# First layer's experts: fourteen scatter-added in memory and two summed on chip, in place of twelve and four

## The chip, the cores and the metric

The kernel runs on one core of a Trainium2 chip. The metric is the device time of one execution in microseconds, as the median of several runs. The core has a matrix engine (TensorE, PE in the rows), a vector engine (VectorE, DVE), a scalar engine (ScalarE, ACT), GpSimd (POOL) and SyncE (SP), which here issues most of the loads. Each engine works through its own list of instructions in order and waits on semaphores for the others. Data move between memory and the on-chip SBUF by DMA; TensorE writes into PSUM, from which VectorE and ScalarE read.

## The reference, cut to what matters

Two layers work on 512 latent tokens and 256 context tokens of width 1024. Each has an attention half and then a mixture of 16 experts in which every expert chooses its own tokens: 64 of the latent and 32 of the context, the context only in the first layer. The expert's rows are scaled and added back into the stream at the chosen places:

```python
def ec_ffn(h, router_w, w_gate, w_up, w_down):
    cap = EC_CAPACITY_FACTOR * n_tok // N_EXPERTS
    aff = jax.nn.softmax((h @ router_w).astype(jnp.float32), axis=-1)
    top_aff, idx = lax.top_k(jnp.swapaxes(aff, 1, 2), cap)
    xg = jax.vmap(lambda hb, ib: hb[ib])(h, idx)
    hid = jax.nn.silu(einsum(xg, w_gate)) * einsum(xg, w_up)
    y = einsum(hid, w_down) * top_aff[..., None].astype(h.dtype)
    return zeros((n_tok, d)).at[idx.reshape(-1)].add(y.reshape(-1, d))
...
xl = xl + g2 * ec_ffn(rmsnorm(xl, norm2_g) * (1 + sc2) + sh2, ...)
```

The context gets the same update (`xc`) in the first layer. The last step of the whole is a norm of the latent stream.

## The kernel before

The change lies in the expert stage of the first layer (`upd` is true there). The stream stands in SBUF as six tiles `X` of 128 tokens by 1024: four latent (`xl`), two context (`xc`). A copy of it was written to memory as `acc` while the tokens were routed (L860).

The experts' weights come through a ring of slots of 1 MB each; SyncE issues the loads, and a slot comes free when TensorE has used it. An expert takes four slots for gate and up (`load_gu`) and two for down (`load_d`).

The loop over `e` from 0 to 16 (L1172) overlaps the experts. One iteration gives TensorE, in this order, which is written out by hand: `gate_up(e, 1)` and `gate_up(e, 0)` (context, then latent rows); `down(e-1, 0)`; the transposes of the next expert's gathered rows (`columns(e+1)`); the transposes of the hidden rows (`hid_t(e, 1)`, `hid_t(e, 0)`), which ScalarE copies to SBUF as `hTe`; up to six pieces of the combine that stood in the list `todo` when the iteration began; `down(e-1, 1)`. The order on the other engines is not written out: a planner sets it, by the order of emission, priorities and its own costs.

What follows `down` differs. For `e < in_dram`, 12 in the first layer, VectorE scales the product's rows into a tile `ya` of 96 rows (two instructions latent, four context), and GpSimd issues a DMA that adds these rows into `acc` at the tokens' places (L1076). For the last four experts the rows are summed on chip. The latent rows become `yt`, and of it `yp`: ScalarE casts the leading part (L1086) and VectorE subtracts it for the remainder (L1087); `yp` has two buffers. GpSimd builds a one-hot tile `pl` of the chosen tokens (`places`, L1103), and TensorE multiplies `pl` with `yp`: each pair of experts gives eight pieces, four token blocks by two halves, of two matmuls each, and VectorE adds each piece into `X` (L1120). The context rows of four experts are gathered in one tile `y` and split into `yc` (`split`), and give four pieces of two matmuls. The pair (12, 13) stands in `todo` from iteration 14 on, so its pieces are multiplied in iterations 15 and 16; the pair (14, 15) and the context come last.

In iteration 14 all of `X` is loaded anew from `acc`, by six DMAs on GpSimd (L1194). A one-column copy of the next expert's `xgT` into each tile (L1193) stands ahead of them, so that they don't run earlier. After the last additions the second layer begins with the norms of the six tiles (L141, L142, L309), which need all of `X`.

Of the kernel before, what the change touches and what calls it, by code (L numbers as in the profile page):

```python
# [10 lines left out]
F32R = mybir.dt.float32r  # L11
# [8 lines left out]
D = 1024  # L20
# [6 lines left out]
NE = 16  # L27
# [17 lines left out]
def hybrid_kernel(ctx: ExitStack, tc: tile.TileContext, a, out):  # L45
    nc = tc.nc
    V, S, G, PE, Q = nc.vector, nc.scalar, nc.gpsimd, nc.tensor, nc.sync

    def early(n):

        def wrap(f):
            def g(*args, **kw):
                with tc.high_priority(n):
                    return f(*args, **kw)
            return g
        return wrap
# [39 lines left out]
    def ps_mm():  # L96
        return psn("mm")

    def ps_tp():
        return psn("tp")  # L100
# [30 lines left out]
    @early(-400)  # L131
    def parts(x, out, hi=None, sub=V):

        (hi or V.tensor_copy)(out[0], x)  # L134
        sub.tensor_tensor(out[1], x, out[0].bitcast(F32), op=OP.subtract)  # L135
# [13 lines left out]
    acc = dram.tile([NT, D], F32, name="acc")  # L149
# [83 lines left out]
    X = {}  # L233

    def layer(li, ada):
        upd = li == 0
# [539 lines left out]
        for r in range(len(streams)):  # L776
            t = rt.tile([128, D], F32, name=f"g1_{r}")
# [6 lines left out]
        for r, grp in enumerate(streams):  # L784
            t = rt.tile([48, len(grp) * 64], F32, name=f"affT{r}")
# [92 lines left out]
        class Choice:  # L878
# [22 lines left out]
            def finish(self):  # L901
                r, cap, np_ = self.r, caps[self.r], nparts[self.r]
                rows = 128 // np_
                v0, v1 = self.val[0:NE], rt.tile([NE, cap], F32, name="mgv")
                V.tensor_copy(v1, self.val[32:48, ::-1])
                lt = rt.tile([NE, 2, 128], F32, name="lt")
                i0, i1, ge = [rt.tile([NE, cap], F32, name=f"mg{i}") for i in range(3)]

                def wide(x):
                    return x[:, None, :].to_broadcast([NE, np_, cap])  # L910

                V.tensor_scalar(i0, self.idx[0:NE], -4.0 * cap, None, op0=OP.add)
                V.tensor_copy(i1, self.idx[32:48, ::-1])
                V.tensor_tensor(ge, v0, v1, op=OP.is_ge)
                V.tensor_tensor(i0, i0, i1, op=OP.subtract)
                V.tensor_tensor(i0, i0, ge, op=OP.mult)
                lw = [lt[:, i].rearrange("p (q c) -> p q c", q=np_) for i in range(2)]
                V.scalar_tensor_tensor(lw[0], wide(i1), 4.0 * cap, wide(i0), op0=OP.add, op1=OP.add)
                V.tensor_tensor(lw[1], wide(v0), wide(v1), op=OP.max)
                ps = ps_tp()  # L920
                for i in range(2):
                    PE.transpose(ps[:, i * NE:(i + 1) * NE], lt[:, i, :], ident[:NE, :NE])

                if r == 1:
                    V.tensor_scalar(gidx[64:96], ps[64:96, :NE], float(NL), None, op0=OP.add)
                    st = mods.tile([128, NE // np_], F32, name=f"st{r}")
                    for q in range(np_):
                        V.tensor_copy(st[q * rows:(q + 1) * rows, :], ps[q * rows:(q + 1) * rows, q:NE:np_])
                else:
                    if upd:  # L930
                        V.tensor_copy(gidx[:64], ps[:64, :NE])
                    else:
                        for q in range(2):
                            V.tensor_copy(gidx[64 * q:64 * q + 64, :NE // 2], ps[64 * q:64 * q + 64, q:NE:2])
                    st = mods.tile([128, NE], F32, name=f"st{r}")
                    V.tensor_copy(st, ps[:, :NE])
                slots.append(st)
                w = mods.tile([128, NE], F32, name=f"gw{r}")
                V.tensor_copy(w, ps[:, NE:2 * NE])
                gw.append(w)  # L940
# [38 lines left out]
        ex = pool(es_x, f"ex{li}", 2, side="right")  # L979
# [9 lines left out]
        xgs, xgTs = {}, {}  # L989
# [65 lines left out]
        Y = {}  # L1055

        def down(e, r):
            wd, hT = wds[e], hTs[e, r]
            ps = ps_mm()
            np_ = nparts[r]  # L1060
            n, rows = D // np_, 128 // np_
            for k in range(4):
                o = k * 64 if r == 0 else (k % 2) * 64 + (k // 2) * 32
                for q in range(np_):
                    mm(ps[rows * q:rows * (q + 1), :n], hT[:, o:o + rows], wd[k][:, q * n:(q + 1) * n], k == 0, k == 3)
            if e < in_dram:

                if r == 0:
                    Y["rows"] = ex.tile([ng, D], F32, name="ya")
                t = Y["rows"]  # L1070
                for q in range(np_):
                    own = slice(rows * q, rows * (q + 1))
                    V.scalar_tensor_tensor(t[64 * r:64 * r + rows, q * n:(q + 1) * n], ps[own, :n], gw[r][own, e:e + 1],
                                           g2[r][own, :], op0=OP.mult, op1=OP.mult)
                if r == 1:
                    G.indirect_dma_start(out=acc, out_offset=bass.IndirectOffsetOnAxis(ap=gidx[:ng, e:e + 1], axis=0),  # L1076
                                         in_=t, in_offset=None, compute_op=OP.add)
                return
            if r == 0:

                t = ex.tile([128, 512], F32, name="yt", bufs=1)
                V.scalar_tensor_tensor(t, ps, gw[0][:, e:e + 1], g2[0], op0=OP.mult, op1=OP.mult)  # L1082
                y = ex.tile([128, 2, 512], F32R, name="yp", bufs=2 if upd else 3)
                for q in range(2):
                    own, other = slice(64 * q, 64 * q + 64), slice(64 - 64 * q, 128 - 64 * q)
                    S.copy(y[own, q], t[own])  # L1086
                    V.tensor_tensor(y[other, q], t[own], y[own, q].bitcast(F32), op=OP.subtract)  # L1087
                Y[0] = y
                return

            i = e % np_
            if i == 0:
                Y[r] = ex.tile([128, D], F32, name=f"y{r}", bufs=1)
            for q in range(np_):
                V.scalar_tensor_tensor(Y[r][i * rows:(i + 1) * rows, q * n:(q + 1) * n], ps[rows * q:rows * (q + 1), :n],
                                       gw[r][rows * q:rows * (q + 1), e:e + 1], g2[r][rows * q:rows * (q + 1), :],
                                       op0=OP.mult, op1=OP.mult)

        def places(r, g):

            nt = NL if r == 0 else NCX
            pl = ex.tile([128, nt], F32R, name=f"pl{r}", bufs=2 - r)
            G.tensor_scalar(pl, tok[:, :nt], slots[r][:, g:g + 1], None, op0=OP.is_equal)  # L1103
            return pl

        def split(g):

            o = [ex.tile([128, D], F32R, name=f"yc{i}", bufs=1) for i in range(2)]
            parts(Y[1], o, S.copy)
            pl = places(1, g)  # L1110
            return [(pl, [y[:, hf * 512:(hf + 1) * 512] for hf in range(2)]) for y in o]

        def combine(r, terms):
# [12 lines left out]
        rs = range(len(streams))  # L1126
        todo, pair = [], []

        in_dram = 12 if upd else 0

        def finish(e, r):
            down(e, r)
# [39 lines left out]
        for e in range(NE + 1):  # L1172
            ready = len(todo)
            if e + 1 < NE and e + 1 not in wgus:
                load_gu(e + 1, G if upd and e == 1 else Q)
            if e < NE:
                if e not in wds:
                    load_d(e, Q if upd or e > 1 else G)
                for r in reversed(rs):
                    gate_up(e, r)  # L1180
            if e and upd:
                finish(e - 1, 0)
            elif e:
                hid_t(e - 1, 0)
            if e < NE:
                if e + 1 < NE:
                    columns(e + 1)
                if e + 2 < NE:
                    gather(e + 2)
                if upd and e == NE - 2:  # L1190

                    for i, t in enumerate(X["xl"] + X["xc"]):
                        V.tensor_copy(t[:, 0:1], xgTs[NE - 1][:, 0, 0:1])  # L1193
                        G.dma_start(t, acc[i * 128:(i + 1) * 128, :])  # L1194
                if upd:
                    for r in reversed(rs):
                        hid_t(e, r)
            fill(min(ready, 6 if upd else 4))
            if e:
                for r in rs[1:] if upd else rs:  # L1200
                    finish(e - 1, r)
        if upd:
            fill(len(todo))
        else:
            final(todo, ex)
# [104 lines left out]
```

## Time and profile before

| what | value |
|---|---|
| time, median of 3 runs | 1432.83 us (1432.7 to 1435.84) |
| time of the profiled execution | 1436.76 us |
| its span, first to last instruction | 1435.0 us |
| mean granted clock of TensorE | 0.958 |
| TensorE busy (matmul) | 1284.1 us, 89% |
| VectorE busy | 710.2 us, 49% |
| ScalarE busy | 513.5 us, 36% |
| GpSimd busy | 216.7 us, 15% |
| moved by DMA | 321.16 MB, 224 GB/s over the span |

The profile is that of one execution, with times from the start of its span. A busy TensorE is not one at its peak, since matmuls are pipelined and their ends modelled. The granted clock is that of TensorE as a share of its full 2.4 GHz. "x96" counts instructions that were merged into one row; a matmul in f32 appears as two. "[2.26 <-ACT hTe L1053]" is idle time of the engine ahead of a row and what ended it.

### The profile page before, as it was taken

What the parts mean: (1) busy time and instruction counts of PE and PEld (TensorE: products, weight loads), DVE (VectorE), ACT (ScalarE), POOL (GpSimd) and SP (SyncE); (2) the same over time, 40 slices, a digit from 0 to 9 for tenths busy, and PEclk for the clock granted to TensorE, in tenths of its full rate; (3) what the DMA queues carried; (4) which work ended last, traced back from release to release, by engine and by line L of the source; (5) the groups of instructions that cost most, each with busy time, mean ns of one, the idle gap of its engine ahead of it and who ended that gap; (6) DMA issues with size and microseconds to landing.
All of it is one profiled execution on the core that took longest, in us unless ns stands there. A gap on an engine that the chain in (4) does not pass through costs nothing. (4 is left out here: it accounts for less than half of the span.)

```text
span 1435.0 us, 21605 instructions
## 1 busy us (share of the span) xinstructions
PE 1284.1 (89%) x8598; PEld 811.0 (57%) x8598; DVE 710.2 (49%) x1564; ACT 513.5 (36%) x1093; POOL 216.7 (15%) x252
## 2 busy tenths in 40 slices
PE   3989989989999959999999959998999968999986
PEld 0768866656678833444443438876778754343332
DVE  1545266566653453333333484847876352333435
ACT  2523145455543322222222143436666232232222
POOL 1111001313120230111110120101232011111201
PEclk9989999999999979999999989999999988999998
DMA  9523416535661389999999610210016447999993
GB/s 359 190 88 118 161 40 235 184 132 195 246 235 54 138 313 363 374 375 376 374 374 389 243 57 32 72 63 1 2 35 258 163 190 303 419 420 419 420 421 124
DMA packets 54084, 321.16 MB, mean 224 GB/s; under 512 B 8528, under 2 KB 8656, under 8 KB 20448
## 3 DMA queue, kind: packets, MB, share of 16 engines
q1 hardware_dynamic: 45664, 286.75, 51.2%
q0 software_dynamic: 8320, 33.03, 7.2%
q8 instruction: 68, 1.11, 0.3%
q14 instruction: 32, 0.26, 0.1%
HBM read 304.52 MB, written 15.24 MB: 223 GB/s over the span
## 5 line engine op out<-in xcount | busy, mean ns | idle before, releaser
L59 PE MATMUL mm<-slot,xgT 128*32 128x256 f32 (+1 forms) x2048 | 289.1, 492 | 5.6 <-DMA slot<-in_exp_w_up_dram 3.9
L59 PE MATMUL mm<-hT,w 128*128 128x512 f32 (+1 forms) x1176 | 228.9, 354 | 3.3 <-POOL w L135 2.0
L59 PEld LDWEIGHTS mm<-hT,w 128*128 128x128 f32 x1176 | 191.4, 191 | 37.1 <-POOL w L135 2.4
L59 PEld LDWEIGHTS mm<-slot,xgT 128*32 128x32 f32 (+1 forms) x2048 | 104.2, 125 | 178.7 <-issue 144.7
L59 PE MATMUL mm<-slot,hTe 128*32 128x256 f32 (+1 forms) x1024 | 150.2, 503 | 0.8 <-ACT hTe L1053 0.8
L1044 DVE TENSOR_TENSOR gh<-mm,gh 64x512 f32<-64x512 f32 (+1 forms) x48 | 29.0, 604 | 226.7 <-ACT gh L1043 225.5
L1043 ACT ACTIVATE gh<-mm 64x512 f32<-64x512 f32 (+1 forms) x48 | 24.9, 519 | 243.1 <-PE mm L59 243.1
L59 PE MATMUL mm<-wo,mixb 128*128 128x512 f32 x360 | 99.1, 411 | 2.3 <-DVE mixb L135 1.3
L1013 ACT ACTIVATE xgT<-tp,modT,a 128x64 f32<-128x64 f32 (+1 forms) x192 | 68.9, 426 | 84.3 <-PE tp L1009 80.9
L59 PEld LDWEIGHTS mm<-slot,hTe 128*32 128x32 f32 (+1 forms) x1024 | 51.1, 126 | 81.5 <-issue 69.1
L689 ACT COPY pt<-tp 128x512 f32<-128x512 f32 (+1 forms) x120 | 64.9, 542 | 82.6 <-PE tp L686 81.4
L686 PE MATMUL tp<-ident,p 128*128 128x128 f32 x552 | 87.4, 284 | 5.5 <-ACT pt L689 2.3
L676 POOL TENSOR_SCALAR p<-p,sm 128x768 f32<-128x768 f32 (+1 forms) x30 | 58.5, 1950 | 124.4 <-DVE sm L675 116.1
L686 PEld LDWEIGHTS tp<-ident,p 128*128 128x128 f32 x552 | 61.5, 142 | 27.8 <-issue 18.7
L59 PE MATMUL ada<-slot,sT 128*32 128x512 f32 x384 | 54.6, 689 | 23.6 <-DMA slot<-in_ada_w_dram 23.6
L59 PEld LDWEIGHTS mm<-wo,mixb 128*128 128x128 f32 x360 | 65.3, 192 | 16.9 <-DVE mixb L135 2.2
L59 PE MATMUL sc<-kt,qh 96*128 96x512 f32 (+1 forms) x324 | 69.7, 348 | 0.0
L134 ACT CAST w<-slot 128x1024 fp32r<-128x1024 f32 x30 | 31.4, 1046 | 100.1 <-PE mm L59 73.8
L59 PE MATMUL sc<-kst,qst 128*128 128x256 f32 (+1 forms) x288 | 48.1, 298 | 20.6 <-DVE mx L673 12.9
L665 DVE TENSOR_REDUCE mx<-sc 128x1 f32<-128x768 f32 (+1 forms) x60 | 51.0, 851 | 26.9 <-PE sc L59 25.9
L996 POOL DMA_INDIRECT xg<-tabx,gidx x24 | 23.2, 968 | 252.4 <-PE tp L1051 149.4
L59 PEld LDWEIGHTS sc<-kt,qh 96*128 96x128 f32 x324 | 52.6, 190 | 10.0 <-issue 3.4
(246 smaller groups left out, 1794.6 us busy)
## 6 DMA issues: line engine op xcount, KB each, us to landing
slot<-in_exp_w_gate_dram SPq DMA_DIRECT2D x62, 1024.0 KB
slot<-in_exp_w_up_dram SPq DMA_DIRECT2D x62, 1024.0 KB
slot<-in_exp_w_down_dram SPq DMA_DIRECT2D x62, 1024.0 KB
slot<-in_ada_w_dram SPq DMA_DIRECT2D x48, 1024.0 KB
slot<-in_win_dram SPq DMA_DIRECT2D x14, 1024.0 KB
slot<-in_wo_dram SPq DMA_DIRECT2D x8, 1024.0 KB
tabx<-xn POOLq DMA_DIRECT2D x10, 512.0 KB, 3.0
xt<-in_x_dram SPq DMA_DIRECT2D x4, 512.0 KB
```

What stands on the lines that cost most here:

```text
L59: PE.matmul(o, l, r, start=start, stop=stop, skip_group_check=True)
L134: (hi or V.tensor_copy)(out[0], x)
L665: V.tensor_reduce(mx, sc[:, :n], axis=AX.X, op=OP.max, negate=True)
L676: (G if s and self.kind == "mla" else V).tensor_scalar(p[:, :n], p[:, :n], sm, None, op0=OP.mult)
L686: PE.transpose(ps[:, b * 128:(b + 1) * 128], p[:, (b0 + b) * 128:(b0 + b + 1) * 128], ident)
L689: S.copy(o, ps[:, :n * 128])
L996: G.indirect_dma_start(out=xg, out_offset=None, in_=tabx[li], in_offset=bass.IndirectOffsetOnAxis(ap=gidx[:ng, c:c + 1], axis=0))
L1013: S.activation(xgT[:, k0 + k, :n], ps[:, k * ng:k * ng + n], AF.Identity, bias=b[:, 0:1], scale=s[:, 0:1])
L1043: S.activation(gh[64:128, :n], ps[0:64, :n], AF.Silu)
L1044: V.tensor_tensor(gh[0:64, :n], ps[64:128, :n], gh[64:128, :n], op=OP.mult)
```

## The change

`in_dram` becomes 14 in the first layer: the rows of experts 12 and 13 are added into `acc` by DMA as well, and only experts 14 and 15 are summed on chip. The context tile `y` is made at expert 14 and only its lower half of partitions (64 to 128) is filled, split and multiplied. The loads of `X` from `acc` move from the middle of iteration 14 to its end, behind `finish(13, 1)`, which issues the scatter of expert 13. They read what that scatter writes and so wait for it. The second layer's path (`in_dram` 0) stays, except that its condition for making the tile is not used there.

```diff
             i = e % np_
-            if i == 0:
+            if e == in_dram:
                 Y[r] = ex.tile([128, D], F32, name=f"y{r}", bufs=1)
...
         def split(g):
 
-            o = [ex.tile([128, D], F32R, name=f"yc{i}", bufs=1) for i in range(2)]
-            parts(Y[1], o, S.copy)
-            pl = places(1, g)
+            o = [ex.tile([128, D], F32R, name=f"yc{i}", bufs=1)[64:128] for i in range(2)]
+            parts(Y[1][64:128], o, S.copy)
+            pl = places(1, g)[64:128]
             return [(pl, [y[:, hf * 512:(hf + 1) * 512] for hf in range(2)]) for y in o]
...
-        in_dram = 12 if upd else 0
+        in_dram = NE - 2 if upd else 0
...
-                if upd and e == NE - 2:
-
-                    for i, t in enumerate(X["xl"] + X["xc"]):
-                        V.tensor_copy(t[:, 0:1], xgTs[NE - 1][:, 0, 0:1])
-                        G.dma_start(t, acc[i * 128:(i + 1) * 128, :])
                 if upd:
                     for r in reversed(rs):
                         hid_t(e, r)
...
             if e:
                 for r in rs[1:] if upd else rs:
                     finish(e - 1, r)
+            if upd and e == in_dram:
+
+                for i, t in enumerate(X["xl"] + X["xc"]):
+                    V.tensor_copy(t[:, 0:1], xgTs[NE - 1][:, 0, 0:1])
+                    G.dma_start(t, acc[i * 128:(i + 1) * 128, :])
         if upd:
             fill(len(todo))
```

## Rows read from the trace of the kernel before

**Rows 1.** The page's slices: mean busy share of the DMA engines, 40 slices.

```profile
DMA  9523416535661389999999610210016447999993
```

**Rows 2.** Windows by iteration; after the length: busy PE, PEld, DVE, ACT, POOL, PEclk, DMA.

```profile
738.50:756.30 17.80, 17.42 (x165) 7.51 (x160) 6.83 (x17) 4.25 (x13) 2.37 (x2) 1.00 1.02 375
756.30:777.80 21.50, 19.24 (x162) 8.16 (x158) 8.51 (x21) 6.05 (x17) 2.37 (x2) 0.89 1.02 379
777.80:799.80 22.00, 19.74 (x163) 8.38 (x158) 7.79 (x23) 5.25 (x14) 3.27 (x6) 0.89 0.94 377
```

**Rows 3.** The same view in finer windows; the last three are PEclk, DMA share, GB/s.

```profile
776.00:778.00 2.00, 2.00 (x24) 0.96 (x20) 0.00 (x0) 0.00 (x0) 0.00 (x0) 0.50 1.04 303
...
788.00:792.00 4.00, 4.00 (x22) 1.40 (x20) 0.69 (x1) 0.59 (x1) 0.00 (x0) 1.00 1.02 426
792.00:794.00 2.00, 2.00 (x16) 0.94 (x12) 0.87 (x2) 0.56 (x2) 0.00 (x0) 1.00 0.88 365
```

**Rows 4.** Timeline of TensorE: start, us, line, operation, out and in, count, idle.

```profile
738.49 10.76 PE L59 MATMUL mm<-slot,xgT 128*32 128x256 f32 x96
...
756.28 10.75 PE L59 MATMUL mm<-slot,xgT 128*32 128x256 f32 x96
...
773.80 0.69 PE L1051 MATMUL tp<-ident,gh 64*128 64x64 f32 x4 [2.26 <-ACT hTe L1053]
...
777.83 11.66 PE L59 MATMUL mm<-slot,xgT 128*32 128x256 f32 x96
...
799.80 10.94 PE L59 MATMUL mm<-slot,xgT 128*32 128x256 f32 x96
...
814.61 3.44 PE L59 MATMUL cb<-yp,pl 128*128 128x512 f32 x12
817.98 5.52 PE L59 MATMUL mm<-slot,hTe 128*32 128x256 f32 x48
823.43 1.20 PE L59 MATMUL cb<-yp,pl 128*128 128x512 f32 x4
824.55 1.93 PE L59 MATMUL mm<-slot,hTe 128*32 128x256 f32 x32
...
830.53 5.50 PE L59 MATMUL cb<-yp,pl 128*128 128x512 f32 x15 [3.62 <-DVE yp L1087]
```

**Rows 5.** Timeline of ScalarE, iteration 13.

```profile
771.62 1.24 ACT L1086 CAST yp<-yt 64x512 fp32r<-64x512 f32 x2
```

**Rows 6.** Timeline of VectorE, the tail of the first layer.

```profile
827.91 0.75 DVE L1082 SCALAR_TENSOR_TENSOR yt<-mm,gw,g2l 128x512 f32<-128x512 f32 x1
828.69 0.98 DVE L1095 SCALAR_TENSOR_TENSOR y<-mm,gw,g2c 32x256 f32<-32x256 f32 x2
829.70 1.40 DVE L1087 TENSOR_TENSOR yp<-yt,yp 64x512 fp32r<-64x512 f32 x2
...
838.76 2.48 DVE L1120 TENSOR_TENSOR xc<-xc,cb 128x512 f32<-128x512 f32 x4 [0.59 <-PE cb L59]
```

**Rows 7.** Timeline of GpSimd: the scatter of expert 11.

```profile
759.61 1.44 POOL L1076 DMA_INDIRECT acc<-ya,gidx  x1 [4.91 <-DVE ya L1073]
```

**Rows 8.** Tile `ya`: from issue to landing of its twelve scatters.

```profile
DMA to landing us min/median/max: 9.1/9.8/10.2
```

**Rows 9.** Tile `acc`: issue of the four latent loads, ns min, median, max.

```profile
L1194 POOL DMA_DIRECT2D xl<-acc x4: 557/568/602, 794.5 to 796.2; - x4
```

**Rows 10.** GpSimd by line, 740 to 860: busy us, mean ns, idle before.

```profile
L1103 POOL TENSOR_SCALAR pl<-tok,st 128x512 fp32r<-128x512 f32 x2 | 3.1, 1566 | 26.8 <-PE cb L59 26.8
```

**Rows 11.** DMA issues, 700 to 860: count, KB each, median us to landing.

```profile
xl<-acc POOLq DMA_DIRECT2D x4, 512.0 KB, 7.6
xc<-acc POOLq DMA_DIRECT2D x2, 512.0 KB, 14.0
```

**Rows 12.** Waits of SyncE's queue, 840 to 1240: us, times, longest.

```profile
SPq L761 <- PE mm L59: 54.3, 8, 26.6
...
SPq L340 <- DVE w L135: 76.0, 4, 26.4
```

**Rows 13.** Line 309, 830 to 860: ns min, median, max of the latent scalings.

```profile
L309 DVE TENSOR_SCALAR xt<-xl,rs_r x4: 752/1790/2843, 842.0 to 850.6; 128x1024 f32<-128x1024 f32 x4
```

## Prediction

> **What bounds the kernel now.** I read first the page's slices, to see where in the span the changed stage lies and what is busy there. The experts of the first layer fill the stretch in which the DMA engines stand at 9 or more tenths, in the middle of the span [rows 1]; TensorE is near full there too, so either could be the limit. The windows by expert settle which: a window is one iteration of the loop, and the iterations in which experts 13 and 14 are multiplied take about 4 us longer than the one before, with TensorE idle for over 2 us and at a lower mean clock, while the DMA share is the same 1.02 [rows 2]. The finer windows show that the DMA engines move over 420 GB/s while no gather or scatter runs, and that the weights' stream runs out at about 794 us, before TensorE even begins expert 15 [rows 3, 4]. So at the end of this stage the weights are ahead, and TensorE's order of work sets the time.
>
> TensorE's own timeline then gives the terms. Expert 13's products start at 756.28, expert 12's had started at 738.49: 17.79 us for an iteration whose predecessor's rows go to memory. Expert 14's start 21.55 us later and expert 15's 21.97 us after that [rows 4]. In both long iterations TensorE waits 2.26 us for the copy of the transposed hidden rows (one of the two stands in the rows), because ScalarE puts the two casts of `yp` (1.24 us) ahead of it [rows 4, 5]; behind the wait the granted clock is 0.50, the lower of its two levels (1.2 of 2.4 GHz), and the next products run long [rows 3]. After the last expert comes a tail: the combine of the last pair, which waits for its `yp` until 830.53, then the context's combine; it ends with four additions into `xc` at 838.76 + 2.48 = 841.24 [rows 4, 6]. The second layer's norms come behind those additions.
>
> **The change part by part.** Experts 12 and 13 no longer form `yt`, `yp` and their one-hot matmuls; they write `ya` and go out by a scatter-add, as experts 0 to 11 do. The loads of `X` move behind the scatter of expert 13.
>
> *Two iterations.* With `down(12)` and `down(13)` in the scattered form nothing stands before the hidden copy, so both iterations should cost what the one before cost: 21.55 - 17.79 = 3.76 and 21.97 - 17.79 = 4.18, together 7.94 us [rows 4]. Expert 15 then starts at 756.28 + 2 x 17.79 = 791.86 instead of 799.80.
>
> *Eight pieces less.* In iteration 15 six pieces of the pair (12, 13) are multiplied, from 814.61 to 817.98, and two more from 823.43 to 824.55 [rows 4]: 3.37 + 1.12 = 4.49 us of TensorE that vanish. They hid nothing that shows otherwise: the hidden copy of expert 15 that the first six cover is then covered by the 32 matmuls of the context's `down(14)`. If ScalarE puts expert 14's casts ahead of that copy, up to 0.6 us comes back.
>
> *The wait on `yp`.* `yp` has two buffers. Today expert 14's can be cast only when the pair (12, 13) has been multiplied, so expert 15's `yt` starts at 827.91, and the combine resumes at 830.53, which is 4.05 us after the last `down` ends (824.55 + 1.93) [rows 4, 6]. In the changed kernel both buffers are free. `yt` takes 0.75, one cast 0.62 and one difference 0.70 [rows 5, 6]: 2.1 us, of which the context's last `down` covers 1.9, so the gap falls to about 0.3 us. If VectorE keeps its present order, in which two context rows `y` (0.98 together) stand before the differences [rows 6], it falls to about 1.8. I take 1.1, the middle: a gain of 3.0, with ends 2.2 and 3.8.
>
> *The rest of the tail.* From 830.53 to 841.24 are 10.71 us: eight pieces, the split of the context's rows, four pieces. Halving the rows of that split does not shorten an instruction whose length goes by its columns, so I keep it; if the difference of the split moves ahead of the latent additions, up to 1.2 comes off.
>
> *What is added.* Two scatters on GpSimd, 1.44 us of issue each [rows 7], where it idles. Two rows of `ya` in place of one `yt` on VectorE lie in the 17.79 already. DMA: two more scatters of 96 rows of 4 KB, 0.8 MB in all; at the rates of [rows 3] some 2 us of the engines, and by an estimate at most 4, if the adding costs as much again. Nothing waits for that: the stream is then done by 798 at the latest, the down weights of expert 15 are wanted after 806.
>
> *The moved loads.* This is the new wait. Expert 11's scatter is issued 3.33 us after expert 13's products start (759.61 against 756.28) [rows 4, 7]; by the same step expert 13's is issued at 795.2. It lands 9.1 to 10.2 us after issue [rows 8], at 804.3 to 805.4, and only then can GpSimd issue six loads of about 0.57 us [rows 9], until 808.8. Behind that wait on GpSimd there could be the one-hot tiles of experts 14 and 15, 1.57 each [rows 10]; even then they are done by 812. The latent tiles landed 7.6 us after issue in the median, the context's 14.0 [rows 11], beside 3 MB of second-layer weights whose loads now come some 8 us earlier. That gives 813.0 (805.4 + 7.6) to 814.7 for the latent tiles, each issued 0.57 behind the other, and 822.2 (808.2 + 14.0) for the context's. In the sum the combine resumes at 791.86 + (814.61 - 799.80) + (823.43 - 817.98) + 1.93 + 1.1 = 815.2, and the context's additions begin 838.76 - 830.53 = 8.2 us later, at 823.4. So the loads are just hidden at the old landing times, and by several us if the earlier weights leave them the engines: 3.1 MB at the 426 GB/s of [rows 3] are 7.4 us.
>
> *Sum.* 3.76 + 4.18 + 4.49 + 3.0 = 15.4 us. The first layer's last addition moves from 841.24 to 825.8. The second layer takes this over whole: SyncE's loads there wait for VectorE and TensorE [rows 12], not for a time of their own. Span 1435.0 - 15.4 = 1419.6, the profiled execution 1436.76 - 15.4 = 1421.4, and from the median of the three runs, 1432.83 - 15.4 = 1417.4.
>
> **The rivals.** *The loads of `X` come late.* For: the chain of scatter, wait and load is new and has 1 us to spare by the worst rows. Two things could lengthen it. If the latent tiles took the 14.0 us of the context's, the fourth would land at 805.4 + 1.7 + 14.0 = 821.1; its first piece, the seventh, is wanted six additions behind the first, at 815.2 + 6 x 0.62 = 818.9 [rows 6], so 2 us are lost. And VectorE and GpSimd can hold each other up: the norms' scaling takes 2.84 us beside GpSimd's splits and 0.75 else [rows 13]. Six issues each held for that difference, 2.1 us, put the fourth at 813.4, and with 14.0 us of landing 8.5 us are lost. Against: the issues took 0.56 to 0.60 us while VectorE was copying and subtracting [rows 9]. Time: 1419.4 to 1425.9.
>
> The Trainium skill (SBUF — State Buffer, SBUF: two separate sides, and the part on the bandwidth-pool intuition in it) goes further than these rows: while VectorE runs an operation that takes the shared port, the descriptors of GpSimd's transfers are not written at all, 3100 ns for one instead of 620. By that the last load would be issued at 821 and land some 4 us late, near 1421. The issue rows of this trace do not show such a hold.
>
> *The weights bind the loop.* Then the two iterations stay long and only the 4.49 and 3.0 remain: 1425.3. For: a DMA share of 1.02 through the loop [rows 2]. Against: the stream runs out 6 us before expert 15 starts. The Trainium skill (DMA: Bandwidth & Descriptors, Specifications) gives about 358 GB/s as a core's share of HBM; six weight tiles and a gather, 6.7 MB in an iteration, would then need 18.7 us, and two iterations would lose 1.8. The trace does not agree: 426 GB/s [rows 3].
>
> *Slower than before.* The place is GpSimd's wait for expert 13's scatter. Were the adding slow to land, all of `X`, and with it every addition, the norms and the second layer, would wait. With 1 us to spare and 15.4 us of gain it turns into a loss when the scatter lands more than 16.4 us later than the 10.2 reckoned with, 26.6 us after issue; at 35 us the time would be 1441. The longest landing in the rows is 10.2 us [rows 8].
>
> *The gain is not handed on.* If the second layer's stream of weights began at a time of its own, the gain would be waited away: 1433.
>
> *More than reckoned.* Additions and split in a better order, and a `yp` that leaves only 0.3 us: 0.8 + 1.2 = 2 us more, and some tenths where the full clock holds through the tail: 1415 to 1413.
>
> **How the numbers follow.** Forecast (1415 to 1419) 0.70; `X` late 0.13; weights 0.05; more 0.05; not handed on 0.03; slower 0.04. The range 1412.5 to 1424.0 holds the forecast, most of the late `X` and the better order, a little over 8 in 10. A measurement of this kernel can tell about 0.3%, 4.3 us, from no change; the weights' case is still beyond that. Faster 0.93, same 0.03, slower 0.04.
>
> **What would show it.** Right: iterations 13 and 14 at 17.8 us with no 2.26 us wait; expert 15 at about 792; no combine between `hid_t(15)` and `down(14, 1)`; the combine's additions never waiting for a DMA; the last `xc` addition ending near 826; the second layer as long as before. Wrong: an idle TensorE whose releaser is a DMA of a weight slot in iterations 14 or 15; VectorE waiting for `xl<-acc`; a GpSimd wait of more than 12 us between scatter and loads; a second layer longer than before.

## The result and the profile after

The changed kernel takes 1421.82 us, the median of 6 runs (1419.62 to 1426.33), beside 1436.16 us for the kernel before on the same chip (6 runs, 1432.7 to 1438.46). The medians lie 14.3 us apart; the ratio is 0.9905, 95% interval 0.9882 to 0.9927, which is a gain of 10.5 to 16.9 us. A second set of 6 runs, which stands as `e6_changed_again` below, gave 0.9928 (0.9905 to 0.9951), with medians 10.8 us apart. The forecast of 1417.4 was too low by 4.4 us; it had the sign right and, as the profiles below show, the place. Of the 30 runs of the kernel before that stood beside the first four experiments one took 5026.67 us and is left out of what follows.

Two times of one kernel differ by several microseconds from run to run, so from here on the place of the change is compared by itself. The span is cut in four: the **front**, up to the first product of expert 13; the **stage**, from there to the end of the last addition into `xc`; the **norms**, from there to the first product of the second layer; and the **rest**. Each cut is a row of TensorE's or VectorE's timeline, in us:

| kernel profiled | front | stage | norms | rest |
|---|---|---|---|---|
| before, the profile of the prediction | 756.28 | 84.96 | 13.59 | 580.2 |
| before, `e10_before_once` | 754.80 | 85.11 | 13.57 | 581.0 |
| before, `e11_before_again` | 757.31 | 85.93 | 13.59 | 582.9 |
| after | 758.35 | 70.86 | 13.59 | 581.8 |
| after, `e6_changed_again` | 753.35 | 71.43 | 13.59 | 581.0 |

Front and rest vary by 3 to 5 us whichever kernel ran, and in these five profiles no effect of the change on either can be seen. The stage repeats to within 1 us, and it is 14.2 us shorter in the mean (85.33 against 71.15).

The windows by iteration of after, with the columns of [rows 2] (length; busy PE, PEld, which is TensorE's loading of weights, DVE, ACT, POOL; PEclk, DMA share, GB/s); the fourth is the end of the tail:

```profile
758.35:776.14 17.79, 17.40 (x163) 7.49 (x159) 6.81 (x17) 4.24 (x13) 2.37 (x2) 1.00 1.02 378
776.14:793.93 17.79, 17.40 (x162) 7.49 (x158) 7.11 (x23) 4.24 (x13) 1.43 (x1) 1.00 1.02 374
...
819.75:829.21 9.46, 7.11 (x18) 4.32 (x18) 8.26 (x13) 6.58 (x11) 0.00 (x0) 0.70 0.05 14
```

Both iterations take 17.79 us, at a granted clock of 1.00 where [rows 2] had 0.89 for the long ones. The DMA share in them is still 1.02.

TensorE's timeline of after, with the columns of [rows 4]:

```profile
758.35 10.75 PE L59 MATMUL mm<-slot,xgT 128*32 128x256 f32 x96
...
773.99 0.46 PE L1051 MATMUL tp<-ident,gh 64*128 64x64 f32 x4 [0.39 <-ACT hTe L1053]
774.39 1.93 PE L59 MATMUL mm<-slot,hTe 128*32 128x256 f32 x32
...
793.93 10.75 PE L59 MATMUL mm<-slot,xgT 128*32 128x256 f32 x96
...
808.56 7.38 PE L59 MATMUL mm<-slot,hTe 128*32 128x256 f32 x80
815.88 2.12 PE L59 MATMUL cb<-yp,pl 128*128 128x512 f32 x6
819.75 4.18 PE L59 MATMUL cb<-yp,pl 128*128 128x512 f32 x10 [1.76 <-DVE xl L1120]
...
825.97 2.51 PE L59 MATMUL cb<-yc,pl 64*128 64x512 f32 x7 [1.61 <-DVE yc L135]
```

The wait of 2.26 us on `hTe` [rows 4] is 0.39. The combine follows the last `down` without a gap (808.56 + 7.38 = 815.94), where before 4.05 us lay between. But it stops after three pieces and waits 1.76 us for VectorE's additions, as it did not before.

VectorE in the same stretch, from the last expert's `yt` to the last addition, to be read beside [rows 6]:

```profile
814.13 0.75 DVE L1082 SCALAR_TENSOR_TENSOR yt<-mm,gw,g2l 128x512 f32<-128x512 f32 x1 [1.04 <-PE mm L59]
815.57 1.40 DVE L1087 TENSOR_TENSOR yp<-yt,yp 64x512 fp32r<-64x512 f32 x2 [0.69 <-ACT yp L1086]
817.01 1.98 DVE L1095 SCALAR_TENSOR_TENSOR y<-mm,gw,g2c 32x256 f32<-32x256 f32 x4
819.01 3.29 DVE L1120 TENSOR_TENSOR xl<-xl,cb 128x512 f32<-128x512 f32 x5
822.47 0.69 DVE L1120 TENSOR_TENSOR xl<-xl,cb 128x512 f32<-128x512 f32 x1 [0.16 <-PE cb L59]
823.32 1.34 DVE L1120 TENSOR_TENSOR xl<-xl,cb 128x512 f32<-128x512 f32 x2 [0.17 <-PE cb L59]
824.69 1.22 DVE L135 TENSOR_TENSOR yc<-y,yc 64x1024 fp32r<-64x1024 f32 x1
826.50 2.71 DVE L1120 TENSOR_TENSOR xc<-xc,cb 128x512 f32<-128x512 f32 x4 [0.59 <-PE cb L59]
```

The durations add up to 13.38 of the 15.08 us from 814.13 to 829.21. Four context rows `y` (1.98) stand ahead of the first addition, which starts 3.1 us after the first piece did. No row waits for a DMA.

GpSimd's timeline of after, the scatter of expert 13 and the four latent loads of `X`:

```profile
797.26 1.42 POOL L1076 DMA_INDIRECT acc<-ya,gidx  x1 [16.36 <-DVE ya L1073]
...
806.96 2.26 POOL L1201 DMA_DIRECT2D xl<-acc  x4 [8.29 <-DMA acc<-ya,gidx]
```

The landing of these four, from the view of the tile `xl`:

```profile
DMA to landing us min/median/max: 5.0/6.3/7.5
```

GpSimd waits 8.29 us for the scatter, and the loads go out 9.7 us after it was issued. The fourth latent tile is issued at 808.6 and so is there by 816.1, 2.9 us ahead of the first addition, which itself came late.

### The profile page after: what moved, and what is told of

Same layout as the page of the kernel before. It is cut to its first block, busy times and chain, and to the rows that moved or that the text cites. A ratio compares the mean times of both kernels' runs of the same rounds, so it can differ in the third digit from the quotient of the medians.

```text
span 1424.6 us, 21563 instructions
## 1 busy us (share of the span) xinstructions
PE 1279.7 (90%) x8582; PEld 813.3 (57%) x8582; DVE 706.0 (50%) x1554; ACT 511.9 (36%) x1089; POOL 216.4 (15%) x252
## 4 chain that ended last, share of the span: by engine, by line
PE 74%; DMA 10%; DVE 9%; ACT 4%; issue 2%; POOL 1%; SPq 0%; POOLq 0%; DVEq 0%; ACTq 0%
PE mm L59 52%; PE sc L59 8%; DMA slot<-in_exp_w_up_dram 4%; PE tp L686 4%; PE ada L59 3%; PE tp L59 2%; DMA slot<-in_exp_w_gate_dram 1%; DMA slot<-in_exp_w_down_dram 1%; DMA slot<-in_ada_w_dram 1%; PE cb L59 1%; PE lg L59 1%; ACT xgT L1013 1%; PE tp L1009 1%; DVE p L673 1%; PE tp L1051 1%
## 5 line engine op out<-in xcount | busy, mean ns | idle before, releaser
L59 PE MATMUL mm<-slot,hTe 128*32 128x256 f32 (+1 forms) x1024 | 147.0, 489 | 0.8 <-ACT hTe L1053 0.8
L59 PE MATMUL ada<-slot,sT 128*32 128x512 f32 x384 | 51.0, 648 | 24.0 <-DMA slot<-in_ada_w_dram 24.0
```

The lines of the kernel that those rows point to most:

```text
L59: PE.matmul(o, l, r, start=start, stop=stop, skip_group_check=True)
```

## The experiments

The theory was that of the prediction: `yp`'s casts and the half clock behind their wait make the two iterations long; the eight pieces and `yp`'s two buffers make the tail long; the loads of `X` are hidden. After the result one more question was open: why the stage gave 1.3 us less than reckoned.

**The casts alone.** The kernel before, with the casts and differences of `yp` emitted behind the hidden copies.

```diff
...
-                for q in range(2):
-                    own, other = slice(64 * q, 64 * q + 64), slice(64 - 64 * q, 128 - 64 * q)
-                    S.copy(y[own, q], t[own])
-                    V.tensor_tensor(y[other, q], t[own], y[own, q].bitcast(F32), op=OP.subtract)
+                def casts():
+                    for q in range(2):
+                        own, other = slice(64 * q, 64 * q + 64), slice(64 - 64 * q, 128 - 64 * q)
+                        S.copy(y[own, q], t[own])
+                        V.tensor_tensor(y[other, q], t[own], y[own, q].bitcast(F32), op=OP.subtract)
+                late.append(casts)
+                if not upd or e == NE - 1:
+                    late.pop()()
...
                         hid_t(e, r)
+                    while late:
+                        late.pop()()
```

> The kernel before (twelve experts scattered, four summed on chip), with one thing changed: the casts and differences that form yp are issued behind the hidden rows' transposes of the same iteration, so that ScalarE copies the first hidden rows before the first cast and the second ones behind one cast only. The stage is measured from the start of expert 13's products to the end of the last addition into xc: 84.96 us before, 70.86 in the changed kernel. Theory (the two long iterations are long because the casts stand ahead of the hidden copy): iterations 13 and 14 fall from 21.55 and 21.97 us to 17.8 to 18.6, the stage to 77 to 78.5, the time by 6.5 to 8 us. Rival (the weights' stream or the number of matmuls sets the iteration): both stay near 21.5, TensorE waiting for a weight slot instead, and the time stays within 1 us.

TensorE's timeline in the iteration of expert 13:

```profile
768.42 0.46 PE L1051 MATMUL tp<-ident,gh 64*128 64x64 f32 x4 [0.38 <-ACT hTe L1053]
770.57 10.73 PE L59 MATMUL mm<-slot,xgT 128*32 128x256 f32 x96
```

The wait is 0.38, and the two iterations take 17.79 and 17.77 us: the place of the two casts on ScalarE, with the differences that hang on them, made up the whole 7.9 us. The stage is 78.07 us, 7.3 below the mean of the three profiles of before. That it is not the full 7.9 lies in the end of the tail, from the combine's last part to the last addition. The window of this kernel:

```profile
819.01:830.85 11.84, 9.30 (x23) 6.50 (x23) 10.22 (x16) 7.32 (x11) 0.00 (x0) 0.64 0.05 11
```

The same stretch in the kernel before, as the prediction had it:

```profile
830.53:841.24 10.71, 7.94 (x23) 4.92 (x23) 9.73 (x16) 7.32 (x11) 0.00 (x0) 0.84 0.03 13
```

And in its last profile, `e11_before_again`:

```profile
831.44:843.24 11.80, 9.14 (x23) 5.69 (x23) 10.10 (x16) 7.32 (x11) 0.00 (x0) 0.71 0.04 11
```

The stretch with the same 23 matmuls is 1.1 us longer at a mean clock of 0.64 or 0.71 than at 0.84, and the kernel before itself shows both. So a tail can be compared to about 1 us, no finer. The times, 1433.35 against 1436.21, ratio 0.9980 (0.9959 to 1.0001), don't by themselves tell this kernel from no change. They miss the 6.5 to 8 us that were expected, and their interval ends at a gain of 5.9 us, below the stage's 7.3. The profile is that of the fastest of the ten runs; what is missing in the others no profile shows.

**The clock alone.** The kernel before, with ten transposes put into the wait, so that TensorE stands idle for less of it.

```diff
+                        if r == 1 and e in (NE - 3, NE - 2):
+                            ps = psn("cb")
+                            for i in range(10):
+                                PE.transpose(ps[:, i % 4 * 128:i % 4 * 128 + 128], ident, ident)
```

> The kernel before with ten extra 128 by 128 transposes (about 1.9 us, their result is not used) in iterations 13 and 14, where TensorE waits 2.26 us for the hidden copy. It separates the wait from the clock. Theory A (of the 3.8 and 4.2 us more that these iterations take, the wait is 1.9 and the rest the lower granted clock behind it): with the array busy the clock stays at 1.00, the down products behind it take 1.9 instead of 3.6 us, the iterations take 19.6 to 19.9, and the time falls by 3.5 to 4.5 us although work was added. Theory B (the products behind the wait are slow for another reason, such as a late operand): the iterations stay at 21.5 or grow, the time by 0 to 2 us.

The products that follow the long wait, on TensorE's timeline of the kernel before:

```profile
774.41 3.64 PE L59 MATMUL mm<-slot,hTe 128*32 128x256 f32 x32
```

The same place in this kernel:

```profile
770.57 1.31 PE L1201 MATMUL cb<-ident 128*128 128x128 f32 x10
772.90 0.46 PE L1051 MATMUL tp<-ident,gh 64*128 64x64 f32 x4 [1.01 <-ACT hTe L1053]
773.29 1.93 PE L59 MATMUL mm<-slot,hTe 128*32 128x256 f32 x32
775.04 10.65 PE L59 MATMUL mm<-slot,xgT 128*32 128x256 f32 x96
```

The window of this iteration, with the columns of [rows 2]:

```profile
755.38:775.04 19.66, 18.64 (x173) 8.56 (x169) 8.51 (x21) 6.06 (x17) 2.37 (x2) 1.00 1.02 381
```

The casts still stand first and the hidden copy comes as late as ever. Yet the granted clock stays at 1.00, the products behind the copy take 1.93 us instead of 3.64, and the iterations 19.66 and 19.56 instead of 21.55 and 21.97. So of the 7.9 us about 3.6 were the wait itself (19.66 + 19.56 - 2 x 17.79) and 4.3 the lower clock behind it. The stage is 81.56, 3.8 below the mean of before. The time, 1435.67, ratio 1.0002 (0.9982 to 1.0022), does not show it: the interval ends at a gain of 2.6 us, short of the stage's 3.8 and of the 3.5 to 4.5 expected. The profiled run's rest came out at 583.7, above the three of before; of the other nine runs there is no profile.

**The buffers of `yp` alone.** The kernel before, with three buffers for `yp` and enough for its one-hot tiles.

```diff
-                y = ex.tile([128, 2, 512], F32R, name="yp", bufs=2 if upd else 3)
+                y = ex.tile([128, 2, 512], F32R, name="yp", bufs=3 if upd else 3)
...
-            pl = ex.tile([128, nt], F32R, name=f"pl{r}", bufs=2 - r)
+            pl = ex.tile([128, nt], F32R, name=f"pl{r}", bufs=(4 if upd else 2) if r == 0 else 1)
```

> The kernel before with three buffers of yp in place of two and four of the latent one-hot tiles, so that expert 14's yp need not wait for the pair (12, 13). Theory (the gap between the last down product and the resumed combine comes from yp's buffers): expert 14's yp is formed before 818, the gap of 4.05 us falls to 0.5 to 2, and the time falls by 2 to 3.5 us. Rival (VectorE's sum of work sets the tail, so that what is formed earlier only pushes the additions of the pair (12, 13) back): the resumed combine starts no more than 1.5 us earlier and the last addition into xc ends less than 1.5 us earlier. Iterations 13 and 14 stay at 21.5 and 22 in either case.

TensorE's timeline at the end of the stage:

```profile
818.40 1.33 PE L59 MATMUL cb<-yp,pl 128*128 128x512 f32 x4 [1.42 <-DVE xl L1120]
...
826.22 1.93 PE L59 MATMUL mm<-slot,hTe 128*32 128x256 f32 x32
828.09 1.65 PE L59 MATMUL cb<-yp,pl 128*128 128x512 f32 x6
831.39 3.13 PE L59 MATMUL cb<-yp,pl 128*128 128x512 f32 x10 [1.65 <-DVE xl L1120]
```

The last additions, on VectorE's:

```profile
837.24 2.66 DVE L1120 TENSOR_TENSOR xc<-xc,cb 128x512 f32<-128x512 f32 x4 [0.59 <-PE cb L59]
```

The wait on `yp` is gone: the combine starts as the last `down` ends. Three pieces later it waits 1.65 us for VectorE, as the changed kernel does. Among the pieces of the pair (12, 13) TensorE waits for VectorE as well, 1.42 us, which it does not in the kernel before. The stage is 83.52, only 1.4 to 2.4 below the three profiles of before, with no edit of anything but buffers. So buffers alone remove the gap of 4.05 us, and 1.6 to 2.6 of it come back, where TensorE now waits for VectorE. The time, 1438.07, ratio 1.0015 (0.9989 to 1.0041), shows a gain of at most 1.6 us, where 2 to 3.5 were expected.

**One expert further.** The changed kernel with fifteen experts scattered and only the last one summed on chip, to put the wait on the scatter where it must show. The part left out here fills a quarter of the context's tile in place of a half.

```diff
...
-        in_dram = NE - 2 if upd else 0
+        in_dram = NE - 1 if upd else 0
```

> The changed kernel taken one expert further: fifteen experts scattered, one summed on chip, the loads of X behind expert 14's scatter. It drives the new wait (scatter lands, then X is loaded, then the additions) onto the path. Theory: the scatter of expert 14 is issued some 19 us after expert 15's products start, lands 9.7 us later, the first tile of X 5 us after that, so VectorE waits for a DMA before the first addition; the last addition into xc ends 5 to 8 us later than in the changed kernel (stage 76 to 79 us), the time 5 to 8 us above it and 6 to 9 below the kernel before. Rival (the landing is hidden here too): the stage is shorter than in the changed kernel by the work of one expert, 1 to 2 us.

GpSimd's timeline:

```profile
811.26 1.40 POOL L1076 DMA_INDIRECT acc<-ya,gidx  x1 [14.14 <-DVE ya L1073]
816.99 2.26 POOL L1201 DMA_DIRECT2D xl<-acc  x4 [4.32 <-DMA acc<-ya,gidx]
```

The first additions on VectorE's:

```profile
820.84 1.28 DVE L1120 TENSOR_TENSOR xl<-xl,cb 128x512 f32<-128x512 f32 x2 [3.41 <-DMA xl<-acc]
```

The window just before the scatter, whose last three columns are PEclk, DMA share and GB/s:

```profile
808.00:811.00 3.00, 3.00 (x30) 1.06 (x24) 2.06 (x5) 0.00 (x0) 0.00 (x0) 1.00 0.03 14
```

Here VectorE does wait for `xl<-acc`, 3.41 us, and the stage is 73.97, 2.8 us longer than the mean of the two profiles of after, although its eight latent pieces are of one matmul each instead of two. The mechanism of the prediction's first rival, `X` coming late, is real; it begins between expert 13 and expert 14. Its size, 5 to 8 us, was overrated: with the DMA engines all but idle (share 0.03 just before) GpSimd went on 5.7 us after the scatter's issue (816.99 - 811.26), not the 9.7 reckoned with. The time is 1428.59, ratio 0.9945 (0.9922 to 0.9968).

**The moved loads alone.** The kernel before, with the loads of `X` at the end of iteration 14 and `in_dram` left at 12.

```diff
-                if upd and e == NE - 2:
-                    for i, t in enumerate(X["xl"] + X["xc"]):
...
+            if upd and e == NE - 2:
+                for i, t in enumerate(X["xl"] + X["xc"]):
```

> The kernel before, twelve experts scattered, with the loads of X issued at the end of iteration 14 as in the changed kernel. One look at the stage, 84.96 us in the kernel before. Theory (the move costs nothing by itself): the loads wait for no scatter any more and are issued within 2 us of expert 15's first products, land before 812, and no addition waits for a DMA; stage 84.5 to 85.5. Rival (moving them puts them on the path even without the scatter): the first additions of the pair (12, 13), which come early here, wait for X, and the stage grows by 1 to 4 us.

GpSimd's timeline:

```profile
795.40 2.22 POOL L1201 DMA_DIRECT2D xl<-acc  x4 [22.09 <-DVE xgT L1015]
```

The planner issues them where it did before (794.5 [rows 9], with a front 0.8 us shorter), ahead of expert 15's products and not within 2 us of them as expected, and the stage is 84.98; the one time taken was 1439.55. So the move in the program is worth nothing by itself; what moves the loads in the changed kernel is the wait for expert 13's scatter.

**VectorE's load in the tail.** The changed kernel, with the difference of `yc` on GpSimd.

```diff
-            parts(Y[1][64:128], o, S.copy)
+            parts(Y[1][64:128], o, S.copy, G)
```

> The changed kernel with one instruction moved: the difference of the context's split yc (1.22 us on VectorE) goes to GpSimd, which idles there. One look at the stage, 70.86 us in the changed kernel. Theory (VectorE's sum of work sets the tail): the last addition into xc ends 1.2 to 1.9 us earlier, stage 69.0 to 69.7. Rival (TensorE's pieces, or the chain from the last down product, set it; or GpSimd's reading of SBUF holds VectorE's additions up): the stage stays within 0.5 us of 70.9 or grows.

GpSimd's timeline, from which VectorE's loses one instruction:

```profile
815.94 2.40 POOL L135 TENSOR_TENSOR yc<-y,yc 64x1024 fp32r<-64x1024 f32 x1 [9.86 <-ACT yc L134]
```

VectorE's, where the context's additions now follow the latent ones at once:

```profile
819.07 1.29 DVE L1120 TENSOR_TENSOR xl<-xl,cb 128x512 f32<-128x512 f32 x2 [0.16 <-PE cb L59]
820.33 2.48 DVE L1120 TENSOR_TENSOR xc<-xc,cb 128x512 f32<-128x512 f32 x4
```

TensorE's, where the wait of 1.61 us for `yc` is gone:

```profile
819.56 2.24 PE L59 MATMUL cb<-yc,pl 64*128 64x512 f32 x8
```

The stage is 68.71, 2.2 and 2.7 below the two profiles of after, where 1.2 to 1.9 were expected, and the one time taken 1421.05. Taking 1.22 us of work from VectorE, and with it the wait of 0.59 that followed, shortens the tail by at least as much: VectorE's queue sets its end. How much of the gain is its sum of work, and how much the chain from its `yc` through TensorE's pieces and back, this run does not separate.

**The changed kernel again, and a better one.** `e6_changed_again` is the changed kernel; `e9_norms_unhindered` adds to the kernel just told of that the second layer's first two splits of weights on GpSimd are planned ahead of the norms.

```diff
-                ws = [win(i, G) for i in range(2)]
+                with tc.high_priority(0 if upd else 600):
+                    ws = [win(i, G) for i in range(2)]
```

> The changed kernel once more, beside the kernel before and the other experiments of this call. It asks whether the gain of its stage, 14.1 us from expert 13's products to the last addition into xc (84.96 to 70.86), is the gain of the whole. Theory (the second layer takes over the whole of it, and what varies lies ahead of the stage): the stage is 70.9 again, the time 13 to 15 us below the kernel before. Rival (some 3 us are given back elsewhere, as the first four experiments' times suggest): the stage is the same and the time only 10 to 11.5 below.

> The changed kernel with the split's difference on GpSimd, as in the other experiment, and with the second layer's first two weight splits, which GpSimd makes, moved ahead of the norms: in both kernels they run beside the scaling of the first two latent tiles (2.84 us each, 0.75 without). Theory (the two engines hold each other up over a shared port and the norms pay 4.2 us): the two scalings take 0.75, and from the last addition into xc to the second layer's first products pass 9.0 to 10 us in place of 13.6; together with the split 5.3 to 6.1 us less than the changed kernel, 19 to 20 less than the kernel before. Rival (the splits hold up the additions instead, or the weights arrive too late to be split there): less than 2 us over the changed kernel.

The first split on GpSimd's timeline of the changed kernel, and the first scaling on VectorE's:

```profile
829.92 2.33 POOL L135 TENSOR_TENSOR w<-slot,w 128x1024 fp32r<-128x1024 f32 x1
...
829.96 2.84 DVE L309 TENSOR_SCALAR xt<-xl,rs_r 128x1024 f32<-128x1024 f32 x1 [0.69 <-POOL rs_r L142]
```

GpSimd's timeline of `e9_norms_unhindered`:

```profile
817.75 4.75 POOL L135 TENSOR_TENSOR w<-slot,w 128x1024 fp32r<-128x1024 f32 x2
```

VectorE's, the last additions and the first scaling of the norms:

```profile
819.70 2.48 DVE L1121 TENSOR_TENSOR xc<-xc,cb 128x512 f32<-128x512 f32 x4
...
823.06 0.75 DVE L309 TENSOR_SCALAR xt<-xl,rs_r 128x1024 f32<-128x1024 f32 x1 [0.82 <-POOL rs_r L142]
```

The splits now run beside the additions, which still follow each other at 0.62 us (four in 2.48, as in [rows 6]), and all four latent scalings of the norms take 0.75 us where two had taken 2.84 [rows 13]. The norms shrink from 13.59 to 9.55 us. Stage and norms together are 6.7 us shorter than in `e6_changed_again`, whose 6 runs were timed beside these: 1418.16 against 1424.83, again 6.7, a little more than the 5.3 to 6.1 expected. Against the kernel before, 1435.64, it is 17.5 us, where 19 to 20 were expected, and the ratio is 0.9882 (0.9859 to 0.9905). It is the fastest version here.

**Was something given back elsewhere?** The medians of the changed kernel were 14.3 and 10.8 us below before, its stage 14.2. Two more profiles of the kernel before were taken to see whether a longer second layer takes part of it.

> The kernel before, unchanged, for a second profile of it: where a run's time spreads outside the stage. Theory (nothing is given back elsewhere): the part before expert 13's products takes 752 to 759 us and the part from the second layer's first products to the end 580 to 584 us, as in the nine profiles so far, so that the changed kernels' 580.9 to 582.8 us are the same spread. Rival (the changed kernels give back 1 to 3 us in the second layer): 579 to 580.5 us again, as the 580.2 of the first profile. The stage itself: 84.96 within 0.2 us by either.

> The kernel before, unchanged, a third time. Theory: 752 to 759 us ahead of expert 13's products, 580 to 584 us behind the second layer's first products, with at least one of the two new profiles above 580.9 us in the latter. Rival: at most 580.5 us in both. The stage: 84.96 within 0.2 us.

The rest of before came out at 581.0 and 582.9, and after's 581.8 and 581.0 lie among 580.2, 581.0 and 582.9: the profiles show nothing given back. The stage of the second one, 85.93, missed its expected 84.96 within 0.2: its two iterations took 21.20 and 21.44, shorter than in [rows 2], and its tail was longer, at the lower clock shown above. The two intervals of the ratio meet at 10.5 to 13.6 us of gain; the stage's 14.2 lies within the first and 0.6 us outside the second. The other sets say more. Only the first set of after gains in time what its stage gains. In the other five sets timed against the kernel before and in the second set of after, the medians gain 3.1 to 4.4 us less than the profile's stage does against the mean of before (in `e9_norms_unhindered` stage and norms), and the stage's gain lies 0.2 to 1.4 us above the end of the interval each time. So some of the gain is missing in the times, and where it goes these profiles, one for each set, do not show.

## Why the prediction was right, and where its sum was off

*What bounds the kernel.* Right. The weights did not bind the loop: at an unchanged DMA share of 1.02 both iterations fell to 17.79 us, moving 378 and 374 GB/s in the mean. The figure of about 358 GB/s (the Trainium skill, DMA: Bandwidth & Descriptors, Specifications), from which the weights' rival had taken its second argument, is not a limit in this trace.

*Two iterations.* Right to the hundredth: 3.76 + 4.18. Expert 15 starts at 793.93; less the 2.07 us by which this run's front is longer (758.35 - 756.28) that is the 791.86 of the sum. The two experiments on the kernel before say why: 3.6 us were the waits and 4.3 the clock behind them.

*Eight pieces less.* Forecast 4.49; from expert 15's start to the end of the last `down` the kernel before takes 799.80 to 826.48, 26.68 us, and after 793.93 to 815.94, 22.01: 4.67. The 0.18 more are expert 15's first products, 10.94 us in [rows 4] and 10.75 in after. The hidden copy was not held up by the casts. No run takes these pieces away alone; the term is read from the rows.

*The wait on `yp`, and the rest of the tail.* This is the term that failed. The forecast let the gap shrink from 4.05 to 1.1 us and kept the 10.71 us behind it. In fact the gap vanished, and what lies behind it grew to 829.21 - 815.94 = 13.27: from the end of the last `down` to the last addition 14.76 us became 13.27, a gain of 1.5 where 3.0 stood in the sum. In the other profiles the same stretch is 14.74 and 15.85 us before and 13.76 after, so no pair of them gains the 3.0 either: it is 1.0 to 2.6.

The main mistake was to price the gap on TensorE alone. In the kernel before VectorE spent TensorE's idle 3.62 us on `yt`, the differences of `yp` and rows `y` [rows 6], and then went on:

```profile
831.14 0.49 DVE L1095 SCALAR_TENSOR_TENSOR y<-mm,gw,g2c 32x256 f32<-32x256 f32 x1
831.66 1.88 DVE L1120 TENSOR_TENSOR xl<-xl,cb 128x512 f32<-128x512 f32 x3
```

Its first addition came 1.1 us after the combine had resumed at 830.53. In after the combine starts earlier, but the differences and the rows `y` have still to be done, and the first addition comes 3.1 us behind it. The bound could nearly all be read from VectorE's timeline before, of which [rows 6] shows the most: from `yt` to the last addition VectorE has 13.38 us of work in after, and the forecast's end (825.8, in this run's time 827.9) left 13.7 us for it, with hardly an idle moment between instructions that wait for TensorE and ScalarE in turn. The runs with more buffers (the same new wait for VectorE) and with the `yc` difference on GpSimd (the tail shorter by more than that difference) bear this out.

A smaller mistake is in the gap itself. The 4.05 us from 826.48 to 830.53 held one matmul of the combine, which TensorE's timeline before shows:

```profile
826.42 0.49 PE L59 MATMUL cb<-yp,pl 128*128 128x512 f32 x1
```

Only 3.62 us were idle. How much of what is missing is the lower clock, 0.70 at the end of after's tail beside 0.84 in the kernel before, no run separates.

*The moved loads.* Hidden, as reckoned, and with more to spare. Expert 13's scatter is issued at 797.26, in the time of before 795.19 against 795.2 reckoned; GpSimd goes on 9.7 us later, within the 9.1 to 10.2 reckoned; the latent tiles land after 6.3 us in the median instead of 7.6 [rows 11], the context's after 9.0 instead of 14.0:

```profile
xc<-acc POOLq DMA_DIRECT2D x2, 512.0 KB, 9.0
```

The Trainium skill's hold of GpSimd's transfers (SBUF — State Buffer, SBUF: two separate sides) did not appear: the six issues took 0.57 to 0.61 us. It was not put to the test either: meanwhile VectorE ran `yt` and the differences of `yp`, none of the copies of which that section speaks.

*The rivals.* The late `X` did not come, and the run with fifteen scattered experts shows that it would have come one expert later. The slower case was far off: the wait was 8.29 us. The second layer took the gain over as far as the profiles show, its norms at the same 13.59 us; the times of the other sets leave some 3 us open, as told above.

*The time.* In the stage 14.1 us (84.96 - 70.86) for 15.4 forecast. The remaining 3 us of the miss are the starting point: the median of three runs, 1432.83, was low beside the 1436.16 of the runs that stood beside the changed kernel; 1436.16 - 14.1 = 1422.1. That this meets the 1421.82 so closely is in part luck: by the same sum the second set should have come out at 1435.64 - 14.1 = 1421.5, and it came out at 1424.83. Nor does the time bear out the mechanism. It lies above the 1415 to 1419 to which the prediction gave 0.70 and within the 1419.4 to 1425.9 of the late `X`, which did not happen; only the profile tells the two apart.

## What to carry to other kernels

A wait that another engine ends costs twice when TensorE's clock falls behind it: price the wait and the longer products after it, and look first whether two casts in another order remove both. Before a gap on one engine is booked as gain, add up the other engine's work in the same stretch: what it did during the gap has to be done afterwards all the same. And a transfer that is moved behind another should be priced from its landing under the load of its new place.

## What the runs showed of the hardware that was not expected

- In the kernel before a wait of 2.26 us was followed by a granted clock of 0.50 and products that took 3.64 us instead of 1.93; in `e2_array_kept_busy`, with the idle time cut to 1.01 us behind ten small transposes, the clock stayed at 1.00.
- A scattered addition of 96 rows let GpSimd go on 9.7 us after its issue with the DMA engines full (a share of 1.03 in the middle of that wait in after, in the row below, whose last three columns are PEclk, DMA share and GB/s), and 5.7 us after it where they had been nearly idle (0.03 just before, in `e5_fifteen_scattered`). It is one such wait each.

```profile
800.00:804.00 4.00, 4.00 (x20) 1.29 (x18) 0.00 (x0) 0.00 (x0) 0.00 (x0) 1.00 1.03 339
```

- GpSimd's subtractions made VectorE's scalings from SBUF to SBUF last 2.84 us instead of 0.75, and did not slow VectorE's additions out of PSUM beside them (four in 2.48 us with or without). The Trainium skill (SBUF — State Buffer, Who interferes with whom) has such a difference: it counts scalar scalings among VectorE's operations that can lock the port shared with GpSimd, and not additions, unless both of their inputs lie in SBUF. The trace agrees.
